# Weight tiles in rings of half blocks, fetched four halves ahead, and a third PSUM bank for the first layer's projections

## The chip, the cores and the metric

The kernel runs on one core of a Trainium2 chip. The metric is the device time of one execution in microseconds, smaller being better. Before the change it was 4348.38 us (median of 3 runs, 4346.02 to 4360.76). An execution that the profiler recorded took 4351.36 us.

## What is computed

A two-layer bidirectional encoder is applied to two sequences, of 512 and 2048 tokens, which the kernel holds one behind the other as 2560 tokens of width 1024. Layer 0 projects the normalised input to 33 x 128 columns. They feed an RWKV-7 recurrence in both directions (8 heads) and a dilated attention (8 heads), each gated by a SiLU path, and one output projection. Layer 1 projects to 24 x 128 + 16 columns for a gated linear attention (GLA, 4 heads, both directions), gate and output projection. Cut to what matters here:

```python
def _even_layer(x, norm_w, w_in, ...):
    p = _rmsnorm(x, norm_w) @ w_in                       # 1024 -> 33 x 128 columns
    shifted = _centred_shift(p[..., :EVEN_SHIFT], mu_prev, mu_next)
    r, k, v, w_lat, a_lat = _split(shifted, ...)
    gate_a, q_b, k_b, v_b, gate_b = _split(p[..., EVEN_SHIFT:], ...)
    y_a = _rwkv7(r, k, v, w_lat, a_lat, ...)
    y_b = _dilated_attention(_rope(heads(q_b)), _rope(heads(k_b)), heads(v_b))
    return x + concat(y_a * silu(gate_a), y_b * silu(gate_b)) @ w_out

def _odd_layer(x, norm_w, w_in, ...):
    p = _rmsnorm(x, norm_w) @ w_in                       # 1024 -> 24 x 128 + 16 columns
    q, k, v, gate_lat, gate = _split(p, ...)
    return x + (_gla(q, k, v, gate_lat, ...) * silu(gate)) @ w_out
```

## The kernel before

**Stages.** From the start to about 1420 us the first layer's projections run (`dense`, L270) beside the preparation of the recurrence (`prep`, L390, with `left` and `inverts`). The tokens go in groups of 512: the first two groups with 13 blocks of 128 columns each, three groups with all 33, then the 20 remaining blocks of the first group. The last 20 blocks (group at token 512) run from about 1420 to 1680 us beside the start of the recurrence (`recurrence`, L642), which goes on beside the attention to 2700 us. Then come the output projection of layer 0, from 2960 to 3940 us the second layer's projections (again `dense`, 5 groups of 25 blocks) mixed with the GLA, and its output projection to the end.

**One block of `dense`.** The product is made in three pieces of reduced precision: the input of a group stands in eight pairs of tiles `xh`, `xl` (high and low part of 128 rows), a block's weights in `wh`, `wl`. One block is 24 matmuls of 128x512 into one PSUM bank `pd`: `wh` with `xh`, `wh` with `xl`, `wl` with `xh`, for each of 8 row groups k. In most blocks the eight `wl` matmuls stand last (`byk` is false).

**Weights.** `wfetch` (L255) loads a block's weights as two halves of 256 KB, `w0` and `w1`, on SP's queue; each has one buffer. `wsplit` (L261) makes the parts: for half 0 VectorE (DVE) casts to `wh` and subtracts to `wl`, for half 1 ScalarE (ACT) casts and GpSimd (POOL) subtracts. `wh` and `wl` hold a whole block and have two buffers each. Both calls for block i+1 stand ahead of the matmuls of block i. Because `w0` and `w1` have one buffer, the load for a block can only be issued when the split of the block before has read it.

**Sinks.** When a block's bank is complete, `even_sink` (L301) or `odd_sink` (L1049) empties it: an ACT copy to `st` (L307, L327), or ACT's tanh to `tmp` and DVE's product to `st` (`silu`, L340 and L341), or two DVE products with the rotary table to `tmp` (L317). `pd` has two buffers, so a block's matmuls can start only when the sink two blocks earlier is done.

**What sets the order.** Each engine runs its instructions in one fixed order, and an instruction that waits holds up all behind it on its engine; SP's queue of DMA issues is such an order too. The program is written as interleaved generators, and the framework's scheduler then fixes each engine's order when the program is built. Buffers come from pools (`open_dense`, L214), and in PSUM `prep` holds 3 banks, `pd` 2 and `pt` (transposes) 2 up to the recurrence, which takes 4 in place of `prep`'s.

Of the kernel before, what the change touches and what calls it, by code (L numbers as in the profile page):

```python
# [11 lines left out]
F32 = mybir.dt.float32  # L12
F32R = mybir.dt.float32r
# [3 lines left out]
OP = mybir.AluOpType  # L17
# [100 lines left out]
class Trunk:  # L118
# [95 lines left out]
    def open_dense(self, es, n):  # L214
        self.xpool = self.pool(es, f"xT{n}", 1)
        self.wpool = self.pool(es, f"w{n}", 2)
        self.stg = self.pool(es, f"st{n}", 2 if n == 0 else 3)
        self.pd = self.pool(es, f"pd{n}", 2, space=PSUM)
        self.pt = self.pool(es, f"pt{n}", 2, space=PSUM)
        self.xes = es.enter_context(ExitStack())  # L220
        self.xr = self.pool(self.xes, f"xr{n}", 2)
        self.xin = self.pool(self.xes, f"xi{n}", 1)
        self._rk = {}
# [28 lines left out]
            yield 430  # L252
        xT[:] = tiles

    def wfetch(self, src, m):  # L255
        ws = [self.wpool.tile([128, 4, 128], F32, name=f"w{h}", bufs=1) for h in range(2)]
        for h, w in enumerate(ws):
            self.nc.sync.dma_start(w[:, :, :m], src[:, 4 * h:4 * h + 4])
        return ws

    def wsplit(self, ws, m):  # L261
        nc = self.nc
        wh, wl = (self.wpool.tile([128, 8, 128], F32R, name=n, bufs=2) for n in ("wh", "wl"))
        for h, (w, e) in enumerate(zip(ws, (nc.vector, nc.gpsimd))):
            k = slice(4 * h, 4 * h + 4)
            (nc.vector.tensor_copy, nc.scalar.copy)[h](wh[:, k, :m], w[:, :, :m])  # L266
            e.tensor_tensor(wl[:, k, :m], w[:, :, :m], wh[:, k, :m].bitcast(F32), op=OP.subtract)  # L267
        return wh, wl

    def dense(self, parts, xT=None):  # L270

        nc = self.nc
        flat = [(p, n, *job) for p, (_, jobs) in enumerate(parts) for n, job in enumerate(jobs)]
        cur = self.wsplit(self.wfetch(*flat[0][2:4]), flat[0][3])
        xT = [] if xT is None else xT
        for i, (p, n, _, m, sink) in enumerate(flat):
            if n == 0 and parts[p][0]:
                yield from parts[p][0](xT)
            wh, wl = cur
            if i + 1 < len(flat):  # L280
                cur = self.wsplit(self.wfetch(*flat[i + 1][2:4]), flat[i + 1][3])
            ps = self.pd.tile([128, 512], F32, name="pd")
            three = [((wh, k, hi), (wh, k, lo), (wl, k, hi)) for k, (hi, lo) in enumerate(xT)]
            byk = n == 0 or n == len(parts[p][1]) - 1
            three = [e for t in three for e in t[:3 if byk else 2]] + [t[2] for t in three if not byk]
            for j, (a, k, x) in enumerate(three):
                nc.tensor.matmul(ps[:m], a[:, k, :m], x, start=j == 0, stop=j == 23)  # L287
                if j % 6 == 5:
                    yield 1280
            sink(ps)  # L290


# [949 lines left out]
    def whole(self):  # L1242
# [4 lines left out]
        def on(side, es):  # L1247

            es.close()
            self.side = side  # L1250
            return es
# [4 lines left out]
        xT = []  # L1256

        def part(t, blocks):

            xT.clear()  # L1260
            return self.dense([(lambda x: self.xeven(x, t), self.even(t, blocks))], xT)
# [8 lines left out]
        for t in (1024, 1536, 2048):  # L1270
            self.mix(part(t, shifted + rest), behind(t - 512), 0.72)
        self.mix(part(0, rest), self.weave(self.inverts(), self.prep(1, 2048), 0.8), 1.0)
        xT.clear()
        self.run(self.xeven(xT, 512))
        self.xes.close()
# [66 lines left out]
```

## Time and profile before

| | us |
|---|---|
| time, median of 3 runs | 4348.38 |
| time of the profiled execution | 4351.36 |
| its span, first to last instruction | 4349.3 |
| TensorE (PE) busy | 3915.0 (90%) |
| DVE busy | 2608.4 (60%) |
| ACT busy | 1774.4 (41%) |
| POOL busy | 1481.2 (34%) |

A busy share is a mean over stages with different limits, so the stages are read one by one below. The end of a matmul is modelled in such a profile: a matmul of 512 columns shows 0.39 us, but the next starts 0.23 us after it. "PEclk" is the granted clock of TensorE: 1.00 is 2.4 GHz, 0.50 is 1.2 GHz, and a value between is a mean over a stretch that has both.

### The profile page before, as it was taken

The numbers are of one execution on the slowest core, as the hardware profiler recorded it, in microseconds if no ns is written. First come the engines' busy times: TensorE is split into PE (matmuls) and PEld (weight loads), VectorE is DVE, ScalarE is ACT, GpSimd is POOL, SyncE is SP. The second block draws the span as 40 slices with busy tenths as digits, with TensorE's granted clock in tenths as the row PEclk, the third lists the DMA queues.
The fourth block names the chain that finished last, engine by engine and source line by source line (L and its number), as shares of the span: only waits on it lengthen the run. The fifth ranks groups of instructions, "written<-read, shape, count | busy, mean of one in ns | idle before, by whom it ended". The sixth has DMA issues, their size and how long they took to land. (4 is left out here: it accounts for less than half of the span.)

```text
span 4349.3 us, 76736 instructions
## 1 busy us (share of the span) xinstructions
PE 3915.0 (90%) x28760; PEld 3050.4 (70%) x28760; DVE 2608.4 (60%) x6092; ACT 1774.4 (41%) x3672; POOL 1481.2 (34%) x1431
## 2 busy tenths in 40 slices
PE   5888789888878898999999997899999999998997
PEld 4666667676656676667776765688777887776776
DVE  3669577686787846545566766323335344567775
ACT  3442434333515234434454544121335344455542
POOL 2454544435545422211122322232333234332331
PEclk9999888989888889778999898999999999999999
DMA  4454444544534545443454443664444444547553
GB/s 146 155 170 150 144 143 160 154 160 147 163 114 138 155 132 150 120 137 108 141 148 131 127 129 103 196 212 138 157 151 153 151 150 133 183 141 233 173 192 125
DMA packets 515503, 653.67 MB, mean 150 GB/s; under 512 B 48188, under 2 KB 340284, under 8 KB 514108
## 3 DMA queue, kind: packets, MB, share of 16 engines
q1 hardware_dynamic: 422044, 560.62, 41.4%
q10 hardware_dynamic: 80464, 72.09, 5.1%
q0 software_dynamic: 12624, 16.06, 1.5%
q8 instruction: 227, 3.72, 0.4%
q14 instruction: 144, 1.18, 0.1%
HBM read 442.48 MB, written 206.36 MB: 149 GB/s over the span
## 5 line engine op out<-in xcount | busy, mean ns | idle before, releaser
L287 PE MATMUL pd<-xh,wh 128*128 128x512 f32 x2320 | 968.9, 420 | 133.3 <-DVE tmp L317 34.7
L287 PE MATMUL pd<-xl,wh 128*128 128x512 f32 (+1 forms) x2320 | 961.4, 415 | 18.9 <-POOL xl L251 18.9
L267 POOL TENSOR_TENSOR wl<-w,wh 128x512 fp32r<-128x512 f32 (+1 forms) x290 | 421.9, 1455 | 936.4 <-ACT wh L266 728.8
L287 PE MATMUL pd<-xh,wl 128*128 128x512 f32 (+1 forms) x2320 | 651.6, 405 | 0.8 <-DVE wl L267 0.8
L287 PEld LDWEIGHTS pd<-xh,wh 128*128 128x128 f32 x2320 | 458.7, 198 | 266.4 <-DVE tmp L317 39.1
L266 ACT CAST wh<-w 128x512 fp32r<-128x512 f32 (+1 forms) x290 | 177.7, 613 | 955.7 <-DMA w<-in_we 533.5
L287 PEld LDWEIGHTS pd<-xl,wh 128*128 128x128 f32 (+1 forms) x2320 | 459.2, 198 | 131.1 <-POOL xl L251 28.0
L287 PEld LDWEIGHTS pd<-xh,wl 128*128 128x128 f32 (+1 forms) x2320 | 442.6, 193 | 100.4 <-issue 4.6
L266 DVE CAST wh<-w 128x512 fp32r<-128x512 f32 (+1 forms) x290 | 148.4, 512 | 461.5 <-DMA w<-in_we 170.0
L267 DVE TENSOR_TENSOR wl<-w,wh 128x512 fp32r<-128x512 f32 (+1 forms) x290 | 247.0, 852 | 110.2 <-PE pd L287 105.0
L1022 PE MATMUL po<-oh,yh 128*128 128x512 f32 x640 | 258.7, 406 | 38.6 <-ACT yh L1011 38.6
L887 ACT ACTIVATE P<-P,O 128x128 f32<-128x128 f32 (+2 forms) x480 | 198.2, 450 | 215.7 <-DVE O L885 209.7
L876 PE MATMUL pS<-Ks,Qs 64*128 64x256 f32 x896 | 270.0, 582 | 6.0 <-DVE O L885 3.2
L1022 PE MATMUL po<-ol,yh 128*128 128x512 f32 x640 | 256.8, 403 | 0.0
L1022 PE MATMUL po<-oh,yl 128*128 128x512 f32 x640 | 251.7, 403 | 2.2 <-DVE yl L1012 2.0
L885 DVE CUSTOM_DVE_ANT_0 P<-pS,msk 128x128 f32<-128x128 f32 (+2 forms) x480 | 153.8, 354 | 144.9 <-PE pS L876 89.0
L925 PE MATMUL pV<-Vt,Pt 128*64 128x65 f32 (+1 forms) x3072 | 184.6, 250 | 32.1 <-DVE O L926 10.2
L925 PEld LDWEIGHTS pV<-Vt,Pt 128*64 128x64 f32 (+1 forms) x3072 | 138.0, 151 | 93.9 <-issue 31.8
L714 POOL TENSOR_TENSOR X<-X,wcs 64x512 f32<-64x512 f32 x76 | 80.3, 1057 | 335.1 <-PE pc L752 171.8
L1009 POOL TENSOR_TENSOR yr<-yr,yg 128x1024 f32<-128x1024 f32 x40 | 97.4, 2435 | 280.9 <-DMA yr<-d_yT 214.1
L876 PEld LDWEIGHTS pS<-Ks,Qs 64*128 64x128 f32 x896 | 148.6, 267 | 52.3 <-issue 13.7
L537 POOL TENSOR_TENSOR PTr<-PTr,wc 128x512 f32<-128x512 f32 x80 | 84.7, 1059 | 258.4 <-PE pg L527 235.7
(280 smaller groups left out, 7709.8 us busy)
## 6 DMA issues: line engine op xcount, KB each, us to landing
w<-in_we SPq DMA_DIRECT2D x330, 256.0 KB
w<-in_wi SPq DMA_DIRECT2D x240, 256.0 KB
d_f<-PT SPq DMA_DIRECT2D x40, 1024.0 KB
PTr<-d_f SPq DMA_DIRECT2D x77, 512.0 KB
d_sg<-st SPq DMA_DIRECT2D x80, 256.0 KB
yr<-d_yT SPq DMA_DIRECT2D x40, 512.0 KB
yg<-d_sg SPq DMA_DIRECT2D x40, 512.0 KB
Vg<-d_gv SPq DMA_DIRECT2D x40, 512.0 KB
```

The lines of the kernel that those rows point to most:

```text
L266: (nc.vector.tensor_copy, nc.scalar.copy)[h](wh[:, k, :m], w[:, :, :m])
L267: e.tensor_tensor(wl[:, k, :m], w[:, :, :m], wh[:, k, :m].bitcast(F32), op=OP.subtract)
L287: nc.tensor.matmul(ps[:m], a[:, k, :m], x, start=j == 0, stop=j == 23)
L537: nc.gpsimd.tensor_tensor(bk, bk, self.wc[:, z, c, :, None].to_broadcast([128, 4, 128]), op=OP.mult)
L714: nc.gpsimd.tensor_tensor(nx, x[lo, 0], self.wcs[:, z, c, :, None].to_broadcast([64, 8, 64]), op=OP.mult)
L876: nc.tensor.matmul(o2, a[o], b[o], start=True, stop=True)
L885: V.tensor_tensor_reduce(P[:, h, :nk], pss[h][:, u, off:off + nk], mask, 1.0, 3e38, op0=OP.add, op1=OP.min, accum_out=m)
L887: nc.scalar.activation(P[:, h, :nk], P[:, h, :nk], AF.Exp, scale=-1.0, bias=m)
L925: nc.tensor.matmul(po[q, h, :], Pt[:r, i, h, q], v[:r, h, :], start=i == 0, stop=i == n - 1)
L1009: nc.gpsimd.tensor_tensor(y, y, g, op=OP.mult)
L1022: nc.tensor.matmul(ps[u][e], a[:, k], b[:, k, c], start=k == 0 and j == 0, stop=k == 7 and j == 2)
```

## The change

`wfetch` and `wsplit` give way to one generator, `weights`, which goes by halves. A raw half `w` has four buffers; four are loaded at the start, and each split of a half is followed by the load of the half four further on. `wh` and `wl` now hold half a block and have three buffers each. `dense` keeps two split halves ahead: at the start of each half's matmuls it asks for the split of the half two further on. Each half's twelve matmuls stand together, so that in most blocks the four `wl` matmuls of half 0 come before the first `wh` matmul of half 1. Which engine splits which half is unchanged.

`pd` gets three banks in the pools opened first (n = 0). Before the recurrence's last 20 blocks the pools are opened anew (n = 2) with two banks; this also loads the rotary table once more. The second layer (n = 1) keeps two. The number of matmuls, casts, subtractions and weight loads is the same.

```diff
     def open_dense(self, es, n):
         self.xpool = self.pool(es, f"xT{n}", 1)
         self.wpool = self.pool(es, f"w{n}", 2)
-        self.stg = self.pool(es, f"st{n}", 2 if n == 0 else 3)
-        self.pd = self.pool(es, f"pd{n}", 2, space=PSUM)
+        self.stg = self.pool(es, f"st{n}", 3 if n == 1 else 2)
+        self.pd = self.pool(es, f"pd{n}", 2 if n else 3, space=PSUM)
         self.pt = self.pool(es, f"pt{n}", 2, space=PSUM)
...
-    def wfetch(self, src, m):
-        ws = [self.wpool.tile([128, 4, 128], F32, name=f"w{h}", bufs=1) for h in range(2)]
-        for h, w in enumerate(ws):
-            self.nc.sync.dma_start(w[:, :, :m], src[:, 4 * h:4 * h + 4])
-        return ws
-
-    def wsplit(self, ws, m):
+    def weights(self, flat):
+
         nc = self.nc
-        wh, wl = (self.wpool.tile([128, 8, 128], F32R, name=n, bufs=2) for n in ("wh", "wl"))
-        for h, (w, e) in enumerate(zip(ws, (nc.vector, nc.gpsimd))):
-            k = slice(4 * h, 4 * h + 4)
-            (nc.vector.tensor_copy, nc.scalar.copy)[h](wh[:, k, :m], w[:, :, :m])
-            e.tensor_tensor(wl[:, k, :m], w[:, :, :m], wh[:, k, :m].bitcast(F32), op=OP.subtract)
-        return wh, wl
+        halves = [(src[:, 4 * h:4 * h + 4], m, h) for _, _, src, m, _ in flat for h in range(2)]
+        raw = []
+
+        def fetch():
+            if halves:
+                src, m, h = halves.pop(0)
+                w = self.wpool.tile([128, 4, 128], F32, name="w", bufs=4)
+                nc.sync.dma_start(w[:, :, :m], src)
+                raw.append((w, m, h))
+
+        for _ in range(4):
+            fetch()
+        while raw:
+            w, m, h = raw.pop(0)
+            wh, wl = (self.wpool.tile([128, 4, 128], F32R, name=n, bufs=3) for n in ("wh", "wl"))
+            (nc.vector.tensor_copy, nc.scalar.copy)[h](wh[:, :, :m], w[:, :, :m])
+            (nc.vector, nc.gpsimd)[h].tensor_tensor(wl[:, :, :m], w[:, :, :m], wh[:, :, :m].bitcast(F32), op=OP.subtract)
+            fetch()
+            yield wh, wl
...
-        cur = self.wsplit(self.wfetch(*flat[0][2:4]), flat[0][3])
+        ws = self.weights(flat)
+        split = [next(ws), next(ws)]
         xT = [] if xT is None else xT
-        for i, (p, n, _, m, sink) in enumerate(flat):
+        for p, n, _, m, sink in flat:
             if n == 0 and parts[p][0]:
                 yield from parts[p][0](xT)
-            wh, wl = cur
-            if i + 1 < len(flat):
-                cur = self.wsplit(self.wfetch(*flat[i + 1][2:4]), flat[i + 1][3])
             ps = self.pd.tile([128, 512], F32, name="pd")
-            three = [((wh, k, hi), (wh, k, lo), (wl, k, hi)) for k, (hi, lo) in enumerate(xT)]
             byk = n == 0 or n == len(parts[p][1]) - 1
-            three = [e for t in three for e in t[:3 if byk else 2]] + [t[2] for t in three if not byk]
-            for j, (a, k, x) in enumerate(three):
-                nc.tensor.matmul(ps[:m], a[:, k, :m], x, start=j == 0, stop=j == 23)
-                if j % 6 == 5:
-                    yield 1280
+            for half in range(2):
+                wh, wl = split.pop(0)
+                split.extend(w for w in (next(ws, None),) if w)
+                three = [((wh, k, hi), (wh, k, lo), (wl, k, hi)) for k, (hi, lo) in enumerate(xT[4 * half:4 * half + 4])]
+                three = [e for t in three for e in t[:3 if byk else 2]] + [t[2] for t in three if not byk]
+                for j, (a, k, x) in enumerate(three):
+                    nc.tensor.matmul(ps[:m], a[:, k, :m], x, start=half == 0 and j == 0, stop=half == 1 and j == 11)
+                    if j % 6 == 5:
+                        yield 1280
             sink(ps)
...
         self.mix(part(0, rest), self.weave(self.inverts(), self.prep(1, 2048), 0.8), 1.0)
+        self.open_dense(on("right", right), 2)
         xT.clear()
```

The build orders the first layer's queues anew. On SP's queue in the third group of tokens, just ahead of the rotary table (`rope`), there stood before (`w` are the weights, `p` the shifted rows of `prep`, `d_rkv` a result of it):

```order
L258 DMA w_4314<-in_we 128x512
L379 DMA p<-d_p 128x513
L258 DMA w_4352<-in_we 128x512
L491 DMA d_rkv<-tq 2x64x512
L258 DMA w_4353<-in_we 128x512
L379 DMA p<-d_p 128x513
L258 DMA w_4395<-in_we 128x512
L258 DMA w_4396<-in_we 128x512
L347 DMA rope<-in_rope 128x2x512
L258 DMA w_4441<-in_we 128x512
L258 DMA w_4442<-in_we 128x512
```

and now (lines are those of the changed file; `d_xt` and `d_f` are results of the preparation):

```order
L265 DMA w<-in_we 128x512 x2
L601 DMA d_xt_94<-XT 128x1024 x2
L388 DMA p<-d_p 128x513
L489 DMA d_f_79<-PT 128x8x256
L265 DMA w<-in_we 128x512 x3
L388 DMA p<-d_p 128x513
L356 DMA rope<-in_rope 128x2x512
L265 DMA w<-in_we 128x512
L500 DMA d_rkv<-tq 2x64x512
L388 DMA p<-d_p 128x513
L265 DMA w<-in_we 128x512 x7
```

The weight loads stand in longer rows, and the table has moved ahead of `d_rkv`. On PE in the second layer a block ended before with the eight matmuls of `wl`, after all sixteen of `wh` (the numbers at `xh` and `xl` count the row groups):

```order
L287 MATMUL pd<-xl_32160,wh 128x512
L287 MATMUL pd<-xh_32161,wh 128x512
L287 MATMUL pd<-xl_32162,wh 128x512
L287 MATMUL pd<-xh_32147,wl 128x512
L287 MATMUL pd<-xh_32149,wl 128x512
L287 MATMUL pd<-xh_32151,wl 128x512
L287 MATMUL pd<-xh_32153,wl 128x512
L287 MATMUL pd<-xh_32155,wl 128x512
L287 MATMUL pd<-xh_32157,wl 128x512
L287 MATMUL pd<-xh_32159,wl 128x512
L287 MATMUL pd<-xh_32161,wl 128x512
L287 MATMUL pd<-xh_32147,wh 128x512
```

and a second half now reads

```order
L296 MATMUL pd<-xh_32625,wh 128x512
L296 MATMUL pd<-xl_32626,wh 128x512
L296 MATMUL pd<-xh_32627,wh 128x512
L296 MATMUL pd<-xl_32628,wh 128x512
L296 MATMUL pd<-xh_32629,wh 128x512
L296 MATMUL pd<-xl_32630,wh 128x512
L296 MATMUL pd<-xh_32631,wh 128x512
L296 MATMUL pd<-xl_32632,wh 128x512
L296 MATMUL pd<-xh_32625,wl 128x512
L296 MATMUL pd<-xh_32627,wl 128x512
L296 MATMUL pd<-xh_32629,wl 128x512
L296 MATMUL pd<-xh_32631,wl 128x512
```

so that `wl` of half 0 is read from the ninth matmul of a block on (before: from the seventeenth), and `wl` of half 1 from the twenty-first as before.

## Rows read from the trace of the kernel before

**Rows 1.** The page: the span, and the granted clock in 40 slices.

```profile
span 4349.3 us, 76736 instructions
PEclk9999888989888889778999898999999999999999
```

**Rows 2.** Busy time by stage; the first line names the columns.

```profile
core 0: us, PE busy (x) PEld busy (x) DVE busy (x) ACT busy (x) POOL busy (x), PEclk, DMA share, GB/s
100.00:420.00 320.00, 274.14 (x1401) 214.54 (x1401) 227.79 (x384) 131.39 (x243) 150.66 (x152) 0.94 0.50 163
420.00:660.00 240.00, 194.32 (x1433) 154.08 (x1433) 164.43 (x260) 92.36 (x176) 108.04 (x103) 0.87 0.45 140
660.00:940.00 280.00, 246.14 (x1679) 195.33 (x1679) 211.41 (x324) 112.66 (x210) 132.16 (x123) 0.90 0.50 158
940.00:1190.00 250.00, 211.55 (x1531) 165.45 (x1530) 178.78 (x266) 100.81 (x191) 124.04 (x121) 0.87 0.50 158
1190.00:1420.00 230.00, 178.83 (x1361) 140.99 (x1361) 179.34 (x268) 88.02 (x167) 115.27 (x110) 0.83 0.41 125
...
2960.00:3940.00 980.00, 966.61 (x4498) 766.99 (x4496) 440.43 (x937) 427.79 (x797) 326.79 (x314) 0.99 0.49 155
```

**Rows 3.** PE's waits, 0 to 1430 us: who for whom, total us, times, longest.

```profile
PE pt L248 <- ACT xr L249: 24.3, 13, 5.9
PE pd L287 <- DVE tmp L317: 23.2, 8, 6.0
PE pd L287 <- DVE st L341: 22.5, 9, 9.4
PE pd L287 <- ACT st L307: 21.0, 12, 3.6
PE pd L287 <- DVE wh L266: 20.9, 7, 8.1
PE pd L287 <- POOL xl L251: 18.3, 15, 3.6
PE pd L287 <- ACT wh L266: 16.4, 3, 6.6
...
PE pd L287 <- DVE wl L267: 0.8, 1, 0.8
```

**Rows 4.** ACT's and DVE's waits for weights, 0 to 1430 us.

```profile
ACT wh L266 <- DMA w<-in_we: 476.7, 107, 13.7
...
DVE wh L266 <- DMA w<-in_we: 160.7, 54, 8.7
```

**Rows 5.** Timeline of SP, ACT and PE around 490 us: start, length, instruction, idle before.

```profile
482.77 0.33 SPq L258 DMA_DIRECT2D w<-in_we  x1
...
493.97 0.62 ACT L266 CAST wh<-w 128x512 fp32r<-128x512 f32 x1 [12.43 <-DMA w<-in_we]
...
494.64 0.79 PE L287 MATMUL pd<-xh,wh 128*128 128x512 f32 x1 [6.58 <-ACT wh L266]
```

**Rows 6.** Timeline of DVE and PE around 783 us.

```profile
782.60 0.43 DVE L266 CAST wh<-w 128x512 fp32r<-128x512 f32 x1 [7.26 <-DMA w<-in_we]
...
784.94 0.79 PE L287 MATMUL pd<-xh,wh 128*128 128x512 f32 x1 [5.99 <-DVE tmp L317]
```

**Rows 7.** Timeline of two blocks of layer 2: PE's block starts, ACT, POOL.

```profile
3139.99 0.39 PE L287 MATMUL pd<-xh,wh 128*128 128x512 f32 x1
...
3145.43 0.39 PE L287 MATMUL pd<-xh,wh 128*128 128x512 f32 x1
...
3137.73 0.62 ACT L266 CAST wh<-w 128x512 fp32r<-128x512 f32 x1 [4.19 <-DMA w<-in_wi]
...
3138.43 1.29 POOL L267 TENSOR_TENSOR wl<-w,wh 128x512 fp32r<-128x512 f32 x1 [3.53 <-ACT wh L266]
```

**Rows 8.** PE's longest wait, 1430 to 1680 us.

```profile
PE pd L287 <- DVE tmp L317: 11.5, 2, 6.6
```

**Rows 9.** Timeline of SP at the start: the first weights.

```profile
12.49 2.66 SPq L258 DMA_DIRECT2D w<-in_we  x2
```

## The prediction, made before the changed kernel ran

> **What bounds the kernel now.** I read the page first, then the busy time by stage, then what PE waits for in each stage, then what the engine that released it had waited for, and last single places in the timeline.
>
> The granted clock [rows 1] is close to full in the second layer's projections and lower in the first 40% of the span. By stage [rows 2], the second layer's projections have PE busy for 966.61 of 980 us at a clock of 0.99: 13.4 us of idle time in all, so hardly anything can be won there. The first layer's projections, 100 to 1420 us, are another matter. Summed over the five rows, PE is busy for 1105 of 1320 us, so it stands still for 215 us, and the clock is 0.94 down to 0.83. No engine is full: DVE has the most beside PE, 962 us.
>
> PE's waits there [rows 3] fall into three kinds. A block's bank is not free (releasers `tmp` L317, `st` L341 and `st` L307, which are sinks): 23.2 + 22.5 + 21.0 = 66.7 us in 29 waits. The first half's or second half's weights are not cast (`wh` L266): 20.9 + 16.4 = 37.3 us in 10 waits. The rest belongs to the input's own preparation and to `prep`. Behind them stands one cause that PE's own list doesn't name: ACT sat idle for 476.7 us in 107 waits, with a cast at the head of its queue whose weights had not landed, and DVE for 160.7 us in 54 [rows 4]. Whatever stood behind that cast, sinks among it, waited too. One place shows it whole [rows 5]: SP issued a half's load at 482.77, ACT's cast of it ran at 493.97, 11.2 us later, after 12.43 us of idling, and PE stood for 6.58 us. Another shows the indirect way [rows 6]: DVE idled for 7.26 us at a cast, the sink's two products came behind it, and PE waited 5.99 us for the bank, not for the weights.
>
> So the bound of this stage is PE with holes, and the holes come from late weights and from sinks that share a queue with them. The clock follows the holes: the 0.83 stands where PE is idle most.
>
> **The change part by part.** Nothing is computed more or less; the counts of matmuls, casts and loads are equal. Everything lies in when things wait. A block of 24 matmuls takes 5.44 us of PE at the full clock (two starts of blocks that follow each other, 3139.99 and 3145.43 [rows 7]).
>
> *Loads four halves ahead.* Before, a load is issued only after the split of the block before, and its flight lies open in front of the next split. Now four halves, two blocks, are in flight or waiting in buffers. Two blocks are at least 2 x 5.44 = 10.9 us, and about 19 us in this stage (145 blocks in some 1370 us are 9.4 us each), against 11.2 us for the slow load of rows 5. So nearly all waits for landing go. What PE gets of it directly: of the 10 waits for `wh`, the three on ACT (16.4 us) and, by the timeline, the two longest of the seven on DVE (8.1 us, and one no longer [rows 3]) had such a load behind them. That is between 24.5 and 32.6 us; I take 30 of the 37.3, with the bounds 16.4 and 37.3.
>
> *The third bank.* It lets a sink come one block later without stopping PE, which is 5.44 us. Of the 29 bank waits the longest two are 9.4 and 6.0 us [rows 3], so at most 3.9 + 0.6 = 4.5 us are left and 62 us go. Some of these go already because the loads are early (rows 6 is one), so the two parts are counted together only once: 30 + 62 = 92 us.
>
> *What is late next.* PE that runs on meets the next thing that isn't ready, chiefly results of ACT, DVE and POOL for `prep` and the transposes (24.3 us of waits for `xr` alone [rows 3]). DVE is 73% busy in this stage and late for reasons other than loads as well, and there the hole moves instead of closing. Bounds: nothing returns, or all 92 us do. I take a third, 30 us, nearer to nothing since ACT, which releases many of these, loses 476.7 us of standing at the head of its queue.
>
> *The clock.* From rows 2, the work lost to the lower clock is (1 - clock) x length: 19.2 + 31.2 + 28.0 + 32.5 + 39.1 = 150 us, and PE is busy for 84% of that, so 126 us against 215 us of idle time: 0.58 us of slow clock for each us of idleness. Bounds: none of it follows, or all in proportion. I take proportion, since the fall stands beside the holes.
>
> *Tighter rings.* `wh` and `wl` now hold three halves where they held two whole blocks. The deadline that moves closest is that of half 0's `wl` (ninth matmul instead of seventeenth), and a split can't start before the half three back has been used. In layer 2, where blocks follow closest, ACT casts half 1 at 3137.73 and POOL is done at 3139.72, 0.27 us before the block begins, and it is read from its 21st matmul, 4.5 us later [rows 7]; the ring's buffer would be free from the middle of the block before, 3139.99 - 2.72 = 3137.27, which is earlier than that cast. So the ring fits there. In the first layer waits for `wl` are 0.8 us today. The nearest row for a POOL result that PE does wait for is `xl`, 18.3 us in 15 waits. Bounds 0 and 18; I take 5.
>
> *Edges.* At the start four halves stand ahead of the input on SP's queue instead of two; two took 2.66 us [rows 9], so +3 us, which nothing hides as PE starts only when the input is there. In the 20 blocks beside the recurrence there are two banks as before, and the 11.5 us of bank waits [rows 8] can lose what late loads add to them; the new pools wait for the old ones' readers and load the table again. Bounds -11 to +10; I take -3. In layer 2 the 13.4 us of idle time bound a gain, and I count 0. SP's queue still holds a load until a buffer is free, with `prep`'s loads and stores behind it; these loads are now early, so I count nothing for it, and if that is wrong it shows as later `p` loads.
>
> **The sum.** Idle time: -92 + 30 + 5 = -57 us; its clock 57 x 0.58 = -33; edges +3 - 3 = 0. Together -90 us against the profiled execution of 4351.4 us, that is 4261. The median of the runs is 3 us below that execution, 4348.4, so the forecast is 4348 - 90 = 4258 us. What a measurement of this kernel can tell from no change is about 0.3%, 13 us.
>
> **The rivals.**
>
> *The bank brings nothing.* PE no longer waits for a bank but, as long, for the results that the same late engine gives next; only the loads pay. For it: DVE is 73% busy, and several sinks in rows 3 are DVE's. Against: PE has blocks to go on with, which need only weights. Then 30 us and their clock (17) are won, 10 us return and 5 are added with their clock (9): 33 us, 4315. The Trainium skill (TensorE: Matmul & The Clock Gate, section "HAM oscillation — how this bites in real kernels") reports a matmul kernel in which, once its engine was kept fed, PSUM double buffering gave no further gain; by that rule the time would be this one. In the trace the engine isn't kept fed: rows 3 have 29 waits for a bank.
>
> *Everything returns.* The stage is bound by the chain through DVE, and its holes only change their names. Then the edges are left and some of the 13 us: about 4345.
>
> *More comes back.* With ACT freed, no third returns, and half of PE's other waits go, 12 of the 24.3 us of `xr` and as much again of `prep`'s, with them: 92 + 24 - 5 = 111 us and 64 of clock, 175: 4173. For it: ACT's 476.7 us. Against: these waits have several causes each.
>
> *The rings starve PE (slower).* Place: the first layer, where ACT and POOL are busiest, and layer 2. If a late subtraction costs PE what `xl` does, 18.3 us for the 48 `xl` of these six groups are 0.38 us each, and two subtractions for each of 145 blocks are 110 us, with the clock 174, and the 90 us above would be overrun: 4348 - 90 + 174 less what I had counted (8), about 4424. It decides from about 0.2 us for each of these 290 halves, where the gain is eaten. Against it: rows 7, and the 0.8 us of rows 3.
>
> **How the numbers follow.** Chances: forecast 0.52 (its own range 4215 to 4300), the bank brings nothing 0.14, everything returns 0.10, more comes back 0.13, the rings starve PE 0.11. The range leaves out the slower rival and a part of the largest gain: 4170 to 4350. Faster by over 0.3%: the forecast, the first and the third of the rivals, 0.79, and I give 0.77 since the order of the dense stages was built anew; within 0.3%: 0.11; slower: 0.12.
>
> **What would show it.** Right: in 0 to 1430 us ACT's waits for `w` below 150 us and DVE's below 60; PE's waits with sinks as releasers below 15 us and for `wh` below 15; the first layer's stage shorter by 70 to 110 us with a clock of 0.9 or more; layer 2's stage still about 980 us with under 25 us of idle time. Wrong: ACT's waits gone but PE's idle time still about 215 us under other names (the bank or everything returns), or new waits of PE for `wl` or for `wh` with PE itself as the releaser of the split (the rings), or later `p` loads behind SP's queue. The recurrence and attention from 1680 to 2700 us, whose order hardly differs, should keep their length within 10 us; if they don't, the change acts through the clock or through what the schedule moved there, and my account has missed it.

## The result, and the profile after

The changed kernel takes 4209.9 us (median of 4 runs, 4195.87 to 4229.88) beside 4351.86 us of the kernel before (4 runs, 4346.02 to 4360.76): a ratio of 0.9676, 95% interval 0.9632 to 0.9719. That is 142 us less; the forecast was 90 us less. The profiled execution's span fell from 4349.3 to 4210.3 us.

The page of the kernel after, span and granted clock in 40 slices, to be read against [rows 1]:

```profile
span 4210.3 us, 76869 instructions
...
PEclk9999999999988878899988987999999999999999
```

The clock is high now from the start up to the attention. For the comparison I cut both traces at five events that every kernel has: the first matmul, the last matmul of `prep`, the attention's first scores, its last product, the last block of the second layer. Busy time by these stages, first of the kernel before (its columns are those of [rows 2]: stretch, length, then busy time of PE, PEld, DVE, ACT, POOL with instructions, clock, DMA share, GB/s):

```profile
38.90:1432.70 1393.80, 1169.20 (x7697) 919.92 (x7697) 1001.58 (x1578) 551.04 (x1030) 661.25 (x635) 0.89 0.47 150
1432.70:1634.30 201.60, 175.36 (x1754) 139.56 (x1753) 133.52 (x202) 53.54 (x115) 67.54 (x63) 0.84 0.48 141
1634.30:2702.60 1068.30, 992.45 (x12059) 736.07 (x12060) 650.97 (x2420) 503.30 (x1303) 252.85 (x272) 0.88 0.44 127
2702.60:3912.30 1209.70, 1174.58 (x5392) 935.26 (x5392) 506.30 (x1017) 456.87 (x822) 388.02 (x339) 0.98 0.51 162
```

and of the kernel after:

```profile
40.50:1307.30 1266.80, 1112.42 (x7653) 886.22 (x7653) 1014.45 (x1570) 551.46 (x1025) 661.54 (x634) 0.93 0.52 165
1307.30:1505.70 198.40, 175.17 (x1790) 140.08 (x1790) 129.84 (x205) 56.54 (x119) 67.37 (x62) 0.91 0.48 146
1505.70:2568.00 1062.30, 990.83 (x12065) 734.76 (x12065) 648.23 (x2421) 502.54 (x1303) 255.19 (x273) 0.87 0.44 128
2568.00:3771.90 1203.90, 1177.71 (x5431) 939.56 (x5430) 517.59 (x1027) 467.67 (x831) 370.65 (x339) 0.99 0.51 162
```

Of the 139 us of span, 127 lie in the first stage, 3 in the second, 6 in the attention and 6 in the second layer; the start and the end are 3 us longer together. Length less PE's busy time is PE's idle time: 224.6 us before and 154.4 after in the first stage. DVE did the same work in a shorter time and is busy for 1014.45 of 1266.80 us, 80% (72% before).

PE's waits from 0 to 1307 us after the change (who for whom, total us, times, longest), against [rows 3]:

```profile
PE pd L296 <- DVE wh L273: 21.3, 13, 4.6
PE pd L296 <- POOL xl L251: 19.2, 11, 4.2
PE pd L296 <- DVE wl L274: 17.4, 12, 5.0
PE pp L497 <- DVE kd L495: 15.6, 8, 4.4
...
PE pd L296 <- DVE st L350: 9.1, 1, 9.1
...
PE pd L296 <- ACT wh L273: 3.6, 1, 3.6
...
PE pt L248 <- ACT xr L249: 2.8, 3, 1.9
...
PE pd L296 <- POOL wl L274: 1.7, 2, 1.5
```

Waits for a bank have fallen from 66.7 us to the one of 9.1. Waits for `wh` fell only from 37.3 to 24.9 us. The waits for `xr` fell from 24.3 to 2.8 us, and waits for `wl` rose from 0.8 to 19.1. ACT and DVE in the same stretch, in front of the casts, against [rows 4]:

```profile
ACT wh L273 <- DMA w<-in_we: 64.0, 10, 13.0
ACT wh L273 <- PE pd L296: 60.6, 38, 7.0
...
DVE wh L273 <- PE pd L296: 42.8, 18, 4.4
...
DVE wh L273 <- DMA w<-in_we: 17.6, 4, 7.6
```

The 476.7 and 160.7 us behind the loads are 64.0 and 17.6 now. The releaser PE has grown from what it was before (0 to 1430 us):

```profile
ACT wh L266 <- PE pd L287: 21.6, 9, 5.6
...
DVE wh L266 <- PE pd L287: 11.1, 4, 6.1
```

Here a cast waits until the matmuls have used up a buffer of the ring. A cast that waits for that is ahead of its reader, and it is the state the change aimed at. One wait has grown that was not meant to: ACT's waits for the shifted rows `p`, which are loaded on SP's queue too, are 52.0 us in the same stretch after 15.4 before. The place of [rows 5] in the kernel after (start, length, instruction, idle before):

```profile
488.43 4.34 SPq L265 DMA_DIRECT2D w<-in_we  x2
...
498.03 0.62 ACT L273 CAST wh<-w 128x512 fp32r<-128x512 f32 x1 [2.87 <-PE pd L296]
```

The load issued first in that pair is the one this cast reads; it was issued 9.6 us ahead of it, and the cast waited for the ring, not for the load.

### The profile page after: what moved, and what is told of

It is laid out like the page before. It is cut to its first block, busy times and chain, and to the rows that moved or that the text cites. A ratio compares the mean times of both kernels' runs of the same rounds, so it can differ in the third digit from the quotient of the medians.

```text
span 4210.3 us, 76869 instructions
## 1 busy us (share of the span) xinstructions
PE 3854.7 (92%) x28760; PEld 3014.9 (72%) x28760; DVE 2620.7 (62%) x6092; ACT 1784.7 (42%) x3672; POOL 1463.5 (35%) x1431
## 5 line engine op out<-in xcount | busy, mean ns | idle before, releaser
L296 PE MATMUL pd<-xh,wh 128*128 128x512 f32 x2320 | 942.5, 409 | 47.4 <-DVE wh L273 21.3
L296 PE MATMUL pd<-xl,wh 128*128 128x512 f32 (+1 forms) x2320 | 942.4, 406 | 20.1 <-POOL xl L251 20.0
L296 PE MATMUL pd<-xh,wl 128*128 128x512 f32 (+1 forms) x2320 | 692.1, 404 | 19.1 <-DVE wl L274 17.4
L274 POOL TENSOR_TENSOR wl<-w,wh 128x512 fp32r<-128x512 f32 (+1 forms) x290 | 400.4, 1381 | 638.7 <-PE pd L296 371.7
L296 PEld LDWEIGHTS pd<-xh,wh 128*128 128x128 f32 x2320 | 446.4, 193 | 164.8 <-DVE wh L273 29.2
L296 PEld LDWEIGHTS pd<-xl,wh 128*128 128x128 f32 (+1 forms) x2320 | 447.7, 193 | 124.9 <-POOL xl L251 26.2
L273 DVE CAST wh<-w 128x512 fp32r<-128x512 f32 (+1 forms) x290 | 167.2, 576 | 354.2 <-PE pd L296 301.1
L274 DVE TENSOR_TENSOR wl<-w,wh 128x512 fp32r<-128x512 f32 (+1 forms) x290 | 238.4, 822 | 64.6 <-PE pd L296 59.4
L934 PE MATMUL pV<-Vt,Pt 128*64 128x65 f32 (+1 forms) x3072 | 184.9, 249 | 19.1 <-DVE O L935 7.4
```

What stands on the lines that cost most here:

```text
L273: (nc.vector.tensor_copy, nc.scalar.copy)[h](wh[:, :, :m], w[:, :, :m])
L274: (nc.vector, nc.gpsimd)[h].tensor_tensor(wl[:, :, :m], w[:, :, :m], wh[:, :, :m].bitcast(F32), op=OP.subtract)
L296: nc.tensor.matmul(ps[:m], a[:, k, :m], x, start=half == 0 and j == 0, stop=half == 1 and j == 11)
L934: nc.tensor.matmul(po[q, h, :], Pt[:r, i, h, q], v[:r, h, :], start=i == 0, stop=i == n - 1)
```

## The experiments

Each kernel was traced once; the times are medians. The table holds what the verdicts below rest on. "Attention at" is the time of the attention's first scores; the idle time is PE's from its first matmul until then; "at half clock" is the time that PE was busy until then while the granted clock stood at 1.2 GHz, by the trace's clock records, and half of such time is lost. Kernels with the same letter ran on one chip, beside the kernel before, whose medians there were 4346.1 (A), 4361.6 (B), 4347.6 (C) and 4357.6 us (D); so ratios of different letters are compared to about 0.4% only.

| kernel (chip) | median us | ratio, 95% interval | attention at | idle | at half clock | attention's length |
|---|---|---|---|---|---|---|
| before | 4351.9 | 1 | 1634.3 | 250.9 | 296.1 | 1068.2 |
| after | 4209.9 | 0.9676 [0.9632, 0.9719] | 1505.7 | 177.6 | 184.5 | 1062.3 |
| e0_after (B) | 4202.1 | 0.9635 [0.9619, 0.9651] | 1506.5 | 174.3 | 189.6 | 1059.9 |
| e4_reopen (A) | 4307.1 | 0.9898 [0.9852, 0.9945] | 1613.9 | 250.9 | 252.0 | 1048.4 |
| e4b_reopen (C) | 4305.3 | 0.9912 [0.9877, 0.9946] | 1615.7 | 251.1 | 245.4 | 1047.8 |
| e1_bank (A) | 4308.4 | 0.9916 [0.9890, 0.9941] | 1597.3 | 231.5 | 246.2 | 1069.1 |
| e1b_bank (C) | 4307.0 | 0.9901 [0.9872, 0.9930] | 1593.7 | 230.1 | 232.7 | 1072.6 |
| e2_rings (A) | 4228.1 | 0.9726 [0.9685, 0.9766] | 1514.3 | 183.5 | 198.5 | 1065.0 |
| e7_nobank (B) | 4221.8 | 0.9695 [0.9667, 0.9723] | 1510.7 | 180.1 | 186.6 | 1066.0 |
| e3_two (A) | 4309.5 | 0.9901 [0.9870, 0.9933] | 1590.2 | 236.9 | 218.5 | 1053.4 |
| e8_two_nobank (B) | 4291.1 | 0.9836 [0.9820, 0.9853] | 1581.2 | 227.8 | 223.2 | 1052.7 |
| e10_three (D) | 4205.8 | 0.9670 [0.9632, 0.9708] | 1510.0 | 174.7 | 202.9 | 1048.9 |
| e6_cast (B) | 4181.0 | 0.9584 [0.9567, 0.9602] | 1467.1 | 152.4 | 155.7 | 1080.1 |
| e9_sub (C) | 4262.7 | 0.9804 [0.9774, 0.9834] | 1547.0 | 210.1 | 204.1 | 1064.1 |

The theories were the prediction's: most of the gain is the bank's (62 of 92 us of waits) and a third of it returns. Against it stood that the bank brings nothing, and that the loads carry more than their own waits.

### One part alone: the bank, or the rings

**e1_bank** is the kernel before with the third bank and the pools opened anew, and the old loads:

```diff
-        self.stg = self.pool(es, f"st{n}", 2 if n == 0 else 3)
-        self.pd = self.pool(es, f"pd{n}", 2, space=PSUM)
+        self.stg = self.pool(es, f"st{n}", 3 if n == 1 else 2)
+        self.pd = self.pool(es, f"pd{n}", 2 if n else 3, space=PSUM)
...
+        self.open_dense(on("right", right), 2)
```

> The kernel before with the third result bank alone (and the pools opened anew before the recurrence); the weights are loaded and split as before. My theory, that both parts act: PE's waits for a bank in the first layer (66.7 us before) fall below 20, ACT's waits for weights stay near 477 us, and the time falls by about 65 us, ratio 0.985 (0.978 to 0.992). Rival, the bank does nearly all of it: ratio 0.970 or less. Rival, the bank brings nothing without early weights: waits for a bank turn into waits for wh, ratio 0.996 to 1.002.

**e2_rings** is the changed kernel without the bank and without the opening:

```diff
-        self.pd = self.pool(es, f"pd{n}", 2 if n else 3, space=PSUM)
+        self.pd = self.pool(es, f"pd{n}", 2, space=PSUM)
...
-        self.open_dense(on("right", right), 2)
```

> The changed kernel with two result banks throughout and without the pools opened anew: the rings and the early loads alone. My theory: ACT's waits for weights in the first layer fall below 120 us, bank waits fall by the share that late loads caused, from 66.7 to about 43 us, and the time falls by about 75 us, ratio 0.983 (0.976 to 0.990). Rival, the loads do nearly all of it: ratio 0.971 or less. Rival, the bank does it: ratio 0.995 or more.

The rings and early loads alone have 2.7 of the 3.2%, 0.9726: more than my theory gave them, and not quite what the rival "nearly all of it" asked for. The bank with the opening has 0.9916. That lies inside my theory's range, but by luck, since the opening has as much without the bank (e4_reopen below). PE's waits in e2_rings, 0 to 1322 us, and then one line of the kernel before, 0 to 1430 us, that [rows 3] leave out:

```profile
PE pp L497 <- DVE kd L495: 29.2, 13, 4.5
PE pd L296 <- DVE tmp L326: 19.0, 8, 4.4
...
PE pt L248 <- ACT xr L249: 6.9, 5, 2.5
...
PE pd L296 <- ACT st L316: 6.2, 5, 3.2
...
PE pd L296 <- DVE st L350: 4.1, 4, 2.1
PE pd L296 <- DVE wh L273: 3.7, 5, 1.7
PE pd L296 <- DVE wl L274: 3.2, 3, 1.6
```

```profile
PE pp L488 <- DVE kd L486: 10.0, 7, 2.8
```

With two banks as before, the waits for a bank are 19.0 + 6.2 + 4.1 = 29.3 us instead of 66.7, and those for `xr` 6.9 instead of 24.3. So more than half of the waits for a bank go without a further bank. How much of that is the earlier loads, and how much the finer halves, e8_two_nobank tells below. Something also came in their place: the waits for `kd`, a result of `prep`, rose from 10.0 to 29.2 us.

### The opening of the pools alone, and the bank beside it

**e4_reopen** is the kernel before with the pools opened anew for the last 20 blocks, and two banks:

```diff
-        self.stg = self.pool(es, f"st{n}", 2 if n == 0 else 3)
+        self.stg = self.pool(es, f"st{n}", 3 if n == 1 else 2)
...
+        self.open_dense(on("right", right), 2)
```

> A control: the kernel before with the pools opened anew ahead of the recurrence, with two banks as before. Only this edge and whatever the scheduler moves after it differ. My theory: ratio 0.997 to 1.003 (I had counted the edge at -11 to +10 us). Rival, that a rebuilt order alone moves this kernel by per cents: outside 0.995 to 1.005.

It has 0.9898, as much as e1_bank, and that is the rival's side: an order built anew moves this kernel by one per cent, with no bank and no earlier load. Since I had not counted that for the opening, both ran again, on another chip:

> e4_reopen once more, beside e1b_bank in one call: the kernel before with the result pool opened again at the recurrence and nothing else. Theory (the 40 us of e4 were a real gain of reopening): ratio 0.985 to 0.995, attention stretch near 1050 us again. Rival (they were the spread of single chips): ratio 0.995 to 1.002, attention near 1068.

> e1_bank once more: the third bank with the old loads. Theory (the bank alone is worth nothing while the weights come late): within 0.4% of e4b_reopen in this call. Rival (it is worth what the bank waits of the kernel before suggest, some 60 us): at least 1% under e4b_reopen.

Both came out as before, 4305.3 and 4307.0 us. The bank, with the old loads, is worth nothing in the time (0.04% between them, each with an interval some 0.6% wide). PE's waits for `pd`, 0 to 1400 us, of e4b_reopen and then of e1b_bank show why:

```profile
PE pd L287 <- DVE tmp L317: 32.0, 10, 5.4
PE pd L287 <- DVE wh L266: 24.2, 9, 6.0
...
PE pd L287 <- DVE st L341: 17.9, 7, 6.9
...
PE pd L287 <- ACT wh L266: 16.7, 3, 6.2
PE pd L287 <- ACT st L307: 13.2, 8, 3.6
```

```profile
PE pd L287 <- DVE wh L266: 51.6, 28, 7.8
...
PE pd L287 <- ACT wh L266: 15.4, 7, 4.4
```

These 63.1 us of waits for a bank have gone, and PE waits 27.4 us more for DVE's `wh`. Up to the attention 21 us of idle time remain won (251.1 to 230.1), and the attention begins 22 us earlier (17 us earlier on chip A). The attention then is 25 us longer, 1072.6 instead of 1047.8 us (stretch, length and busy time, then the clock, as above; first e4b_reopen, then e1b_bank):

```profile
1615.70:2663.50 1047.80, 984.78 (x12065) 729.97 (x12065) 649.45 (x2422) 503.30 (x1303) 256.12 (x273) 0.89 0.45 130
```

```profile
1593.70:2666.30 1072.60, 996.03 (x12065) 741.92 (x12066) 651.12 (x2422) 502.95 (x1303) 254.95 (x273) 0.86 0.44 127
```

PE's busy time at half clock is 229.9 us there in e4b_reopen and 280.1 in e1b_bank, and its idle time 63.0 and 76.6 us. The program of this stage is the same in both kernels, and so is the number of instructions, but the build has ordered them anew: at least 51 of DVE's 2421 instructions and 42 of ACT's 1303 stand at another place, while the runs of one kernel on two chips agree in all of them. One such place in DVE's order, again first e4b_reopen:

```profile
1733.37 0.17 DVE L209 TENSOR_TENSOR rsu<-rsu,va 128x16 f32<-128x16 f32 x1
1733.46 0.29 DVE L926 COPY O<-pV 128x130 f32<-128x130 f32 x1
```

```profile
1714.10 0.17 DVE L209 TENSOR_TENSOR rsu<-rsu,va 128x16 f32<-128x16 f32 x1
1714.31 0.17 DVE L210 SCALAR_TENSOR_TENSOR rsy<-rsu,rsy 128x16 f32<-128x16 f32 x1
```

So the bank's gain ahead of the attention is shown, and what takes it back is not: it can be the order in the attention, or the clock, or both.

The opening alone begins the attention 19 to 20 us earlier, and the attention itself, again in another order, is 20 us shorter than in the kernel before. Up to the attention the idle time is the same (250.9 us in the kernel before, 250.9 and 251.1 with the opening), but 44 to 51 us less of the busy time are at half clock, which is 22 to 25 us. Some 25 of the 44 to 51 us lie before 1200 us, where DVE, ACT and POOL have nearly the same order in both kernels. There is only one trace of the kernel before, so how much of this is the opening's doing was not settled.

### The bank beside early loads

**e7_nobank** is the changed kernel with two banks (the pools are still opened anew), and **e0_after** the changed kernel once more, beside it:

```diff
-        self.pd = self.pool(es, f"pd{n}", 2 if n else 3, space=PSUM)
+        self.pd = self.pool(es, f"pd{n}", 2, space=PSUM)
```

> The changed kernel with two banks instead of three in the first layer, all else kept (rings, loads four ahead, pools opened anew): what the third bank is worth on top of early loads. The bank alone and the pools opened anew alone came out alike (0.9916 and 0.9898), while in the first layer's stage of their profiles the bank had 30 us less. If the bank is worth something on top of the rings: 10 to 30 us slower than the changed kernel, ratio to the kernel before 0.970 to 0.975, and bank waits of PE back at about 30 us. If it is worth nothing: ratio 0.966 to 0.970.

> The changed kernel again, unedited, on the chip on which the others of this call run: an anchor. Ratio 0.963 to 0.972 as measured first; if it lies elsewhere, differences of the single edits below 0.5% are not to be read.

4221.8 against 4202.1 us: the changed kernel with the third bank is 20 us, 0.5%, faster than with two, as told. Little of that is seen in the bank's own stage: the attention begins 4 us earlier, and PE's idle time until then is 174.3 instead of 180.1 us. The two traced executions lie 12 us apart, 4 up to the attention, 6 in it and 2 after it, and in the attention at least 129 of DVE's 2421 instructions stand at another place. So some 4 us can be put down to the bank, and the rest may come from the order built anew. PE's waits for a bank were 37.4 us in e7_nobank and 9.1 in the changed kernel; nearly all of the difference came back under other names, the waits for `wl` among them (3.2 us in e7_nobank, 19.1 in the changed kernel). Up to the attention the opening is worth some 3 us beside early loads (e2_rings 1514.3, e7_nobank 1510.7, on two chips), not the 20 it gave alone.

### How far ahead

**e3_two** is the changed kernel with two raw buffers and two halves ahead; **e8_two_nobank** the same on e2_rings; **e10_three** with three:

```diff
-                w = self.wpool.tile([128, 4, 128], F32, name="w", bufs=4)
+                w = self.wpool.tile([128, 4, 128], F32, name="w", bufs=2)
...
-        for _ in range(4):
+        for _ in range(2):
```

> The changed kernel with two raw buffers instead of four, and two halves loaded ahead: rings of three split halves and the third bank stay. If the distance of the loads is what counts, ACT's waits for weights in the first layer come back to 200 us or more and 30 to 60 us of the 142 us won are lost: ratio to the kernel before 0.975 to 0.982. If the finer rings and the bank are what counts, the ratio stays within 0.4% of the changed kernel's 0.968.

> Split halves in rings of three, raw halves only two ahead, two banks, pools not opened anew: the finer rings by themselves. Against e2_rings it differs in the distance of the loads alone. If the distance carries the gain: ACT's waits for weights in the first layer over 300 us, the stage within 20 us of the kernel before, ratio 0.993 to 1.003. If the finer grain carries it: ratio below 0.985.

> The changed kernel with three raw buffers and three halves ahead, between the changed kernel (four, ratio 0.9635 to 0.9676) and e3_two (two, 0.9901). Theory (the distance has to outlast one slow load, 11.2 us; two halves are on average 9.4 us of this stage, three are 14): nearly all of the gain is there with three, ratio 0.964 to 0.971, ACT's waits for raw weights fall from 329.9 us in e3_two to under 130. Rival (loads queue behind other transfers for longer than that, and each half further helps alike): half-way, ratio 0.975 to 0.982, ACT's waits near 200 us.

With two ahead, about 70% of the gain is gone with the bank (1.0% is left of 3.2 to 3.7; the single runs of e3_two spread from 4286 to 4343 us), more than I had told, and 40% without it (1.6% is left of e2_rings' 2.7); with three it is all there. ACT's waits for loads, 0 to 1400 us of e3_two, then 0 to 1307 us of e10_three:

```profile
ACT wh L273 <- DMA w<-in_we: 329.9, 80, 13.1
```

```profile
ACT wh L273 <- DMA w<-in_we: 131.1, 35, 13.3
```

The page's list of DMA issues (queue, count, size, median us from issue to landing) of e3_two, then of e10_three:

```profile
w<-in_we SPq DMA_DIRECT2D x330, 256.0 KB, 3.3
```

```profile
w<-in_we SPq DMA_DIRECT2D x330, 256.0 KB, 3.2
```

A load takes the same 3.2 to 3.3 us (median of the 38 and 43 loads whose landing the trace tells), so it is not the transfer that changed. Pairing each of the first 290 loads with its cast, both in queue order, the median from issue to cast is 4.5 us in the kernel before, 5.0 with two ahead (e3_two and e8_two_nobank alike), 8.3 with three and 11.3 with four. At two, that is only 1.7 us more than the median landing, and every slow load shows; single waits of some 13 us remain in all three.

But the distance is not the whole cause. e8_two_nobank came out below 0.985, on the side that I had named for the finer grain, although ACT waits 342.9 us for loads in it (0 to 1400 us) and its loads are hardly earlier than before. Against the kernel before, its rings of halves begin the attention 53 us earlier with 23 us less of PE's idle time (250.9 to 227.8); another 15 us of its gain lie in the attention, whose order was built anew. From there to e2_rings the programs differ in the distance alone, and the attention begins 67 us earlier with 44 us less of idle time (to 183.5). PE's waits for a bank in e8_two_nobank, 0 to 1400 us:

```profile
PE pd L296 <- DVE tmp L326: 28.5, 10, 6.2
PE pd L296 <- DVE st L350: 20.9, 11, 3.2
...
PE pd L296 <- ACT st L316: 4.7, 4, 3.0
```

They are 54.1 us, after 66.7 before and 29.3 in e2_rings: 25 us of waits for a bank go with the distance of the loads alone, where the banks are two in both. There the sink was late because a cast ahead of it in its engine's queue had no weights. Why the rings of halves gain at the old distance was not tested. Nor do the parts add up: with the bank and the opening, two halves ahead are worth no more than the opening alone (e3_two 0.9901, e4_reopen 0.9898, one chip).

ACT's 131.1 us with three, against 64.0 with four, cost nothing in the time: 0.9670 and 0.9635 to 0.9676. Idle time of ACT matters to PE only while it delays a result that PE comes to next.

### What is late next

After the change DVE is 80% busy in the stage, and most of PE's waits name it. **e6_cast** gives both halves' casts to ACT:

```diff
-            (nc.vector.tensor_copy, nc.scalar.copy)[h](wh[:, :, :m], w[:, :, :m])
+            nc.scalar.copy(wh[:, :, :m], w[:, :, :m])
```

> The changed kernel with both halves' casts on ScalarE (half 0's was on VectorE). In the changed kernel VectorE is busy for 80% of the first layer's stage and releases most of PE's remaining waits there (wh 21.3, wl 17.4, kd 15.6, st 9.1, kk 6.7 us); ScalarE is at 44%. If VectorE is what is late next, taking 145 casts of 0.43 to 1.5 us from it shortens the stage by 25 to 55 us: ratio to the kernel before 0.955 to 0.962. Rival, ScalarE's queue, which waits for PE and VectorE in turn, delivers the casts no sooner: ratio 0.966 to 0.975.

4181.0 us beside 4202.1 of e0_after on the same chip, ratio to before 0.9584, the fastest of all. Busy time from 0 to 1269 us, and the largest of PE's waits there after the start:

```profile
0.00:1269.00 1269.00, 1098.66 (x7643) 879.90 (x7643) 935.97 (x1446) 641.31 (x1185) 648.86 (x645) 0.94 0.52 169
```

```profile
PE pd L296 <- DVE wl L274: 25.6, 16, 4.3
```

The attention begins 39 us earlier than in e0_after, and half of this is lost again in the attention (1080.1 against 1059.9 us, with 282 instead of 228 us of busy time at half clock; its order was built anew here, too). **e9_sub** takes the subtractions from DVE too:

```diff
-            (nc.vector, nc.gpsimd)[h].tensor_tensor(wl[:, :, :m], w[:, :, :m], wh[:, :, :m].bitcast(F32), op=OP.subtract)
+            nc.gpsimd.tensor_tensor(wl[:, :, :m], w[:, :, :m], wh[:, :, :m].bitcast(F32), op=OP.subtract)
```

> e6 with the subtractions of both halves on GpSimd, so that VectorE keeps only its additions, copies and sinks. Theory (VectorE, busy 75 to 80% of the first-layer stage, is what TensorE now waits for): VectorE's share falls to about 65%, TensorE's waits for wh and wl of VectorE (25.6 us in e6) fall under 10, the stage is 10 to 40 us shorter than e6's 1229, ratio to before 0.949 to 0.956. Rival (the subtractions merely move the wait): GpSimd, 53% busy, rises to 65 to 70%, TensorE waits for GpSimd's wl instead, the stage stays at 1220 to 1260 us, ratio 0.957 to 0.966.

It is slower by more than the rival allowed, 0.9804. Busy time and PE's waits, 0 to 1357 us:

```profile
0.00:1357.00 1357.00, 1135.78 (x7704) 899.05 (x7704) 925.66 (x1302) 647.74 (x1193) 856.05 (x801) 0.92 0.50 160
```

```profile
PE pd L296 <- POOL wl L274: 28.0, 15, 5.6
...
PE pd L296 <- ACT wh L273: 13.3, 5, 5.3
```

DVE fell to 68%, and its `wl` is off the list, but POOL, at 63%, is late in its place, and so is ACT, whose casts now wait 47.5 us (0 to 1260 us) for POOL to give buffers back. A share of 63% was no room to spare: POOL takes 1.30 us (median) for a subtraction that DVE does in 0.69. DVE won little in return. 144 instructions fewer ran on it in the stage, but its busy time fell only from 935.97 to 925.66 us: its other instructions, the same in kind and number, took some 107 us longer in sum than in e6_cast, while ACT's kept their lengths (0.2 us in sum).

## Why the prediction was right, and where its sizes were not

**The direction and the place** were right: 128.6 of the 139 us were won before the attention, by less idle time of PE and a higher clock. Of the signs that I named, ACT's and DVE's waits for loads (64.0 and 17.6 us, below 150 and 60), the bank waits (9.1, below 15), the clock (0.93), the second layer's idle time (15.8 us in the 980 us from 2837 on that answer to the last of [rows 2]) and the attention's length (6 us less) came as told. The waits for `wh` did not (24.9 us, 15 expected), two signs of being wrong appeared (waits of PE for `wl`, 0.8 to 19.1 us, and later `p` loads, 15.4 to 52.0 us of ACT's waits, for which I had counted nothing; what they cost in the time no run tells), and the stage shortened by 127 us where 70 to 110 were given. About 10 of the 127 are 1.8 blocks of 5.44 us that now run after the last `prep` matmul.

**Loads and bank, −92 with +30 returned and +5 for the rings.** The sum of idle time was −57 and became −70 in the stage: bank waits −57.6, `wh` −12.4, `xr` −21.5, `wl` +18.3 make −73.2. The total was near, and its split between the parts was wrong. I gave 62 us to the bank because PE's list names the sink. e2_rings reaches 154.4 us of idle time in the stage without a third bank, the same as the changed kernel. So the loads' term of 30 should have been about 70 together with the rings (21 of it with e8_two_nobank's rings of halves, 49 with the distance), and the bank's about 0 in idle time beside early loads. With late loads the bank does win idle time, 17 us of the stage's (e4b_reopen to e1b_bank), for 63 us of waits. [rows 6] had shown the indirect way in one place; the step that failed is that I took it for one wait among 29, not for the rule.

**What returns.** A third was taken of both. The runs tell the parts apart. Of the bank's own gain nearly all returned beside early loads (37.4 us of bank waits in e7_nobank, 6 us of idle time less with the bank), and some two thirds with late ones. Of the gain of loads and rings a fifth did: in e2_rings the waits for banks, `wh` and `xr` fell by 87 us and the idle time of the stage by 70, with `kd` up by 19. The waits for `xr` fell by 17 to 21 us, where the rival "more comes back" had 12; the time lies between the forecast and that rival.

**The clock, 0.58 us for each us of idleness.** In the first stage busy time at half clock fell by 238.4 − 151.7 = 86.7 us, worth 43 us for 70 us of idleness, 0.62. Up to the attention it is 56 us for 73, 0.76. The mean ratio of the stage before was a fair price for the first stage, and too low for the last 20 blocks, whose clock rose from 0.84 to 0.91 with hardly less idle time (26.2 to 23.2 us). That the clock is a matter of idle time alone is not borne out: e4_reopen has 22 us of it without any change of idleness. My reading of [rows 1] left out that the two lowest slices, 1740 to 1957 us, lie in the attention, for which the sum has no term; and the order there, which I said hardly differs, was built anew (at least 270 of DVE's some 2420 instructions stand at another place). Its length changed by 6 us only, but builds of this series range from 1048 to 1080 us, so that this sign came true by luck.

**The rings, 5 us with 0 to 18 as bounds.** PE waits 19.1 us for `wl` in the changed kernel, but 3.5 us in e2_rings and 3.2 in e7_nobank, which have the same rings and two banks. So these waits come with the third bank and are its returned gain; the rings' own cost is no more than the 5 us I took. What I had not counted is that they gain as well, some 20 us of idle time with the loads two halves ahead (e8_two_nobank). The second layer did not starve: it is 6 us shorter.

**Edges.** The start cost 1.6 us, 0.6 in e0_after (+3 told; the four loads take 4.95 us on SP's queue instead of the 2.66 of [rows 9]). The opening of the pools was worth some 3 us up to the attention beside early loads, as I had counted, but 40 us in the whole time alone, which no row had shown.

**The rival that the bank brings nothing** was nearly right about the bank, and its time was wrong since it let the loads pay only for their own waits. (Its sum has a slip as well: 47 us won less 24 is 23, so 4325 and not 4315.) The Trainium skill (TensorE: Matmul & The Clock Gate, section "HAM oscillation — how this bites in real kernels") reports that PSUM double buffering brought no further gain in a kernel whose TensorE was kept fed. By the time of the whole it looks the other way round here: 2 us, no difference that can be measured, with late loads (e4b_reopen, e1b_bank), and 20 us, 0.5%, with early ones (e7_nobank, e0_after). Up to the attention, where the bank acts, the traces agree with it better: the third bank wins 17 to 22 us with late loads and 4 us with early ones, where PE is idle less.

## What to carry to other kernels

A wait is listed under the engine that released it; before a cost is given to a buffer, look at what the releasing engine itself had waited for, since one late load at the head of an in-order queue shows as waits for banks, transposes and weights alike. Fetch so far ahead that the slow loads are covered, not the median one: here the step from two halves to three was worth 2.3% of the time, and that from three to four nothing. Test each part of a change by itself, at the old distance too: rings of halves gained 1.6% with loads that were hardly earlier. When the holes are closed, the busiest engine that stands between load and matmul is next, and moving work off it pays only onto an engine whose own results are not waited for (casts to ACT: 21 us won; subtractions to POOL as well: 2.2% lost). And where each build orders the engines anew, compare stage by stage: opening pools anew gave 1% here, and the attention, whose program is the same in all kernels, differed by up to 32 us between them.

## What the runs showed of the hardware that was not expected

DVE was slower beside POOL: in the first stage of the changed kernel its cast of a half took 0.43 us on average where no TENSOR_TENSOR instruction ran on POOL at the same time (98 casts) and 1.00 us where one did (50; a longer cast is also likelier to meet one). In e9_sub, with all subtractions on POOL, DVE's other instructions took the 107 us longer told above, and ACT's did not. So DVE's busy share depended on what POOL was given.

The same number of matmuls of the attention, 12065, took 1047.8 us in one kernel and 1072.6 in another, at clocks of 0.89 and 0.86, and each kernel gave nearly its own length again on another chip (1048.4 and 1069.1). The programs differ only ahead of the attention, but the engines' orders in it differ as well. So a gain in one stage can be given back in a later one that the edit does not name: e1b_bank lost 25 us in this way, e6_cast 20. Whether the order, the clock or the two together decide it stays open.
